# Weight buffers kept through the output projection, the first pair's weights loaded during it, and banks of their own for its first products

## The chip, the cores and the metric

The kernel runs on one core of a Trainium2 chip. The metric is the device time of one execution in microseconds (us); lower is better. The tensor engine is called PE, the vector engine DVE, the scalar engine ACT, GpSimd POOL, and SyncE, which here only issues transfers, SP.

## What is computed

One layer of a decoder step for 512 prompt rows and 8 x 4 sample rows, 544 columns in all, in 32-bit floats. The parts that matter here, cut from the reference:

```python
def mixer_block(h, pos, gla_s0, k_hist, v_hist, w_in, w_gate_up, b_gate, gla_norm, w_out):
    q_a, k_a, v_a, r_a, z_a, q_b, k_b, v_b = split_in_proj(h @ w_in)
    o_a, s_fin = gla_recurrence(...)
    gate = jax.nn.silu(r_a...)
    o_a = (rmsnorm(o_a, gla_norm) * gate)
    o_b = dilated_attention(...)
    y = jnp.concatenate([o_a, o_b], axis=-1) @ w_out

def conv_ffn(h, conv_hist, w_up, conv_w, conv_b, w_down):
    up = h @ w_up
    conv = conv_b + (causal convolution of width 3 over up)
    u, g = conv[..., :D_FF], conv[..., D_FF:]
    return (jax.nn.silu(g) * u) @ w_down

hp = hp + mixer(rmsnorm(hp, norm_mix));  hp = hp + conv_ffn(rmsnorm(hp, norm_ffn));  y = rmsnorm(hp, norm_final)
```

D_MODEL is 2048, D_FF 5504, w_in 2048 x 6160, w_out 2048 x 2048, w_up 2048 x 11008, w_down 5504 x 2048.

## The kernel before

Everything lies feature-major: a tile is 128 features by 544 columns, which `hv` shows as two halves of 272. A product is made of three matmuls of 128x272 per 128x128 block of weights: operands are split into a high part that the engine's fast 32-bit form keeps exactly and a low rest (`split`: ACT copies the high part, DVE subtracts), and high x high, high x low and low x high are added up (`gemm`, L225). Weights come in units of eight blocks: SP loads them into a `raw` buffer, ACT makes `whi` (L190), DVE `wlo` (L191).

The stages run one after the other:

- **Mixer.** Products with w_in, tile by tile, with the two attentions between them. Weight units lie in the pool `wts` (`raw`, `whi` and `wlo` with three buffers each; `wunit`). The last tiles are the gates of the heads (`in_tile(C_RA + ...)`, evaluated at L373 and in `silu_neg`); the last chunk of the gated attention (L762 to L769) ends at the same time, and L805 multiplies both.
- **Output projection.** `o` is split into `og` (L190, L191: `ah`, `al`), sixteen output tiles of two units each are multiplied, k in the order 10 to 15, 0 to 9, so that the heads finished last come last. Each tile is added to x (POOL loads x), written to `hscr` by POOL, squared for the norm's sum (L905, L906) and scaled (L908). Weight units lie in a second pool, `wu`, which is opened when `wts` is closed (L810, L811), with three `raw` and four `whi` and `wlo` buffers.
- **Factors and norm.** From two scaled tiles, `factors` builds the operands of a fast scheme for 2x2 blocks, which needs seven products where the plain one needs eight: `v` (L877) and `vh`, `vl` (L869, L870). The first four pairs of tiles are done as the projection goes, the last four after it (L914). `rms_stat` makes the norm's factor (L325 on PE, L167 to L171) in the banks of `pss`.
- **Up projection.** 43 pairs of tiles (`Pair`). For each, SP loads `ra` and `rs` into a pool `ra` with two buffers, POOL adds a second half of weights to them on the way in (L968), and further units go through `wraw`. `p1` is a product with plain 32-bit matmuls (L943), the other six are split ones (L938), into banks `b0` (two), `z` (two) and `y` (two) of the pool `psu`. That pool is opened when the norm's pool `pss` and the projection's `psg` are closed (L916, L920). The pools `ra` and `vb` take the place of `acts`, the split activations, and open when the projection is through (L911).
- **Down projection.** The last three finished pairs are kept on the chip and multiplied first, 18 matmuls for each of 16 output tiles, and ACT copies the result out (`h<-g`, L1129): the *kept phase*. The other 40 row tiles come back from memory in groups of 16, 16 and 8 (`fetch`, split by ACT and DVE as `dh`, `dl`). The last eight output tiles of the last group are done by halves, so that the final norm of one half can run beside the products of the other (`finish`, L1194; L1221 multiplies by the norm's factor). Its banks are new pools: three pairs `g`, two `v`.

Each engine runs its instructions in one fixed order. That order is made when the kernel is built, from priorities: code inside `high_priority` (`wpart`, `ahead`) is moved forward by up to a set distance. A buffer is given out again when all who used it have finished, and a pool that is opened in the place of another waits for the users of that other one.

Of the kernel before, what the change touches and what calls it, by code (L numbers as in the profile page):

```python
# [9 lines left out]
F32 = mybir.dt.float32  # L10
F32R = mybir.dt.float32r
U8 = mybir.dt.uint8
AF = mybir.ActivationFunctionType
OP = mybir.AluOpType
AX = mybir.AxisListType
PSUM = bass.MemoryType.PSUM

P = 128
D = 2048
KD = D // P  # L20
TP = 512
NB = 8
TS = 4
NS = NB * TS
NT = TP + NS
HT = NT // 2
NIN = 6160
C_QA, C_KA, C_VA, C_RA, C_Z, C_QB, C_KB, C_VB = 0, 640, 1280, 2560, 3840, 3856, 4624, 5392
RANK = 16
# [6 lines left out]
KF = FF // P  # L36
# [8 lines left out]
NKEPT = 3  # L45
NSLOT = 11
FW = 2 + TP + NB * (2 + TS)
# [62 lines left out]
NVEC = 54 + 258 + 86  # L110
# [13 lines left out]
def _build(tc, nc, es, xT, st_gla, ck, cv, conv_in, vecs, w_in, w_gu, w_out, w_up, w_dn,  # L124
           t_cs, t_bp, t_masks, t_scan, t_small,
           yT, gla_p, gla_s, kT_p, k_s, vT_p, v_s, conv_out):
    def opened(*args, **kw):
        p = tc.tile_pool(*args, **kw)
        return p, p.__enter__()

    def closed(*pools):
        for p in pools:
            p.__exit__(None, None, None)
# [25 lines left out]
    b_x = small[:NS, P + 25:P + 25 + TS * NB].rearrange("p (t b) -> p t b", t=TS)  # L159
    onesD = cons.tile([P, P], F32, name="onesD")  # L160
    eps = cons.tile([P, 1], F32, name="eps")
    zs = cons.tile([2 * RANK, NT], F32, name="zs")
    rstd = cons.tile([P, NT], F32, name="rstd")

    def rsqrt(dst, src, x, r):
# [71 lines left out]
    def ttile(name, dt=F32):  # L237
        return PA.tile([P, NT], dt, tag="T", name=name, bufs=5)

    phase = {"attention": True, "scores": False, "units": 0}  # L240
    nc.scalar.preload_act_table_set("natural_log_exp_and_others")
    xg = []
    acc = ttile("acc")
# [53 lines left out]
    def gps():  # L297
        return pg.tile([P, 2, 512], F32, tag="g", name="g")
# [4 lines left out]
    def vps():  # L303
        return pS.tile([P, 512], F32, tag="v", name="v", bufs=1)
# [502 lines left out]
    gl.__exit__(None, None, None)  # L807
    pe.__exit__(None, None, None)

    closed(wts_p)  # L810
    wu_p, wu = opened(name="wu", bufs=1, side="right")  # L811


    def wsplit(raw, n=8):

        hi = wu.tile([P, 8, P], F32R, tag="whi", name="whi", bufs=4)
        lo = wu.tile([P, 8, P], F32R, tag="wlo", name="wlo", bufs=4)
        split(hi[:, :n], lo[:, :n], raw[:, :n])
        return hi, lo

# [19 lines left out]
        return [(k, hi[:, i, :], lo[:, i, :]) for i, k in enumerate(ks)]  # L840

    def wraw():
        return wu.tile([P, 8, P], F32, tag="raw", name="raw", bufs=3)

    order = [10, 11, 12, 13, 14, 15, 0, 1, 2, 3, 4, 5, 6, 7, 8, 9]
    og = [None] * KD
# [3 lines left out]
    closed(rb2, rowsB_p, rowsA_p)  # L850

    va_p, VA = opened(name="va", bufs=1, side="right")
    hx_p, HX = opened(name="hx", bufs=1, side="right")
    hscr = [dram.tile([P, NT], F32, name=f"hscr{k}") for k in range(KD)]
    adr = [dram.tile([P, NT], F32, name=f"adr{k}") for k in range(KF)]
# [35 lines left out]
    for ot in range(KD):  # L891
# [17 lines left out]
        if j == 1 and i < AHEAD:  # L909
            factors([i], X, VA)  # L910
    closed(acts_p)  # L911
    ra_p, RA = opened(name="ra", bufs=2)
    vb_p, VB = opened(name="vb", bufs=1)
    factors(list(range(AHEAD, KD // 2)), X, VB)  # L914
    rms_stat(acc2, rstd, htmp)
    closed(hx_p, pss, psg)  # L916

    g0_p, G0 = opened(name="g0", bufs=NKEPT, side="right")
    fp_p, FP = opened(name="ffn", bufs=1, side="right")
    psu_p, pu = opened(name="psu", bufs=1, space=PSUM)  # L920
    rstdF = FP.tile([P, FW], F32, name="rstdF")
    nc.vector.memset(rstdF, 1.0)
    nc.scalar.activation(rstdF[:, 2:2 + TP], rstd[:, :TP], AF.Copy)
    nc.scalar.activation(rstdF[:, 2 + TP:].rearrange("p (b s) -> p b s", s=2 + TS)[:, :, 2:],
                         rstd[:, TP:].rearrange("p (b t) -> p b t", t=TS), AF.Copy)
    vcv = FP.tile([P, NVEC - V_CW], F32, name="vcv")
    nc.gpsimd.dma_start(vcv, vecs[:, V_CW:])
    wv = w_up.rearrange("(k t p) c -> t p k c", t=2, p=P)
    NP = TP - HT

# [12 lines left out]
            nc.tensor.matmul(b[:, :HT], a[:, i, :], v11[i], start=(i == 0), stop=(i == 7), skip_group_check=True)  # L943

    def tmp(name):
        return FP.tile([P, HT], F32, tag=name, name=name, bufs=1)

    def second(F, a, b):

        nc.vector.tensor_add(F[:, 2 + HT:2 + TP], a[:, :NP], b[:, :NP])  # L950
        nc.vector.tensor_add(F[:, 2 + TP:].rearrange("p (b s) -> p b s", s=2 + TS)[:, :, 2:],
                             a[:, NP:HT].rearrange("p (b t) -> p b t", t=TS), b[:, NP:HT].rearrange("p (b t) -> p b t", t=TS))

    class Pair:

# [3 lines left out]

        def load(self, *parts, tag=None):  # L960

            x = RA.tile([P, 8, P], F32, tag=tag, name=tag) if tag else wraw()
            for n, (side, t) in enumerate(parts):
                c0 = side * FF + self.f * P
                if n == 0:
                    nc.sync.dma_start(x, wv[t][:, :, c0:c0 + P])
                else:
                    nc.gpsimd.dma_start(x, wv[t][:, :, c0:c0 + P], accum_op=OP.add)  # L968
            return x
# [9 lines left out]
        def p5(self):  # L979
            with ahead():  # L980
                self.s = self.load((1, 0), (1, 1), tag="rs")
                A = wsplit(self.s)
            self.z = pu.tile([P, 512], F32, tag="z", name="z", bufs=2)
            product(self.z, A, T1)

        def p6(self):
# [7 lines left out]
        def p2(self):  # L994
            with ahead():
                self.a12 = self.load((0, 1))
                A = wsplit(self.a12)
                nc.vector.tensor_add(self.s, self.s, self.a12)
            y = pu.tile([P, 512], F32, tag="y", name="y", bufs=2)
            product(y, A, B21)  # L1000
            self.Fu, self.Fg = [FP.tile([P, FW], F32, tag="F", name="F", bufs=2) for _ in range(2)]
            for s, F in enumerate((self.Fu, self.Fg)):
                nc.gpsimd.memset(F[:, 0:2], 0.0)
                nc.scalar.activation(F[:, 2 + TP:].rearrange("p (b s) -> p b s", s=2 + TS)[:, :, 0:2],
                                     self.ci[:, s].rearrange("p (b r) -> p b r", r=2), AF.Copy, scale=(1.0, -1.0)[s])
            nc.vector.tensor_add(self.Fu[:, 2:2 + HT], y[:, :HT], self.V)
# [25 lines left out]
        def conv(self):  # L1032
# [12 lines left out]
                out.append(c)  # L1045
            return out

    ci_v = conv_in.rearrange("p (s f) r -> p s f r", s=2)
    co_v = conv_out.rearrange("p (s f) r -> p s f r", s=2)
    def sv(x):  # L1050
# [2 lines left out]
    KEPT = list(range(KF - 1 - NKEPT, KF - 1))  # L1053
    kept = {}
    ci = co = None
    pairs = [Pair(f) for f in range(KF)]
    for f, pr in enumerate(pairs):
        if f % 4 == 0:
            n = min(4, KF - f)
# [1 line left out]
            co = FP.tile([P, 2, 4, 2 + 2 * NB], F32, tag="co", name="co", bufs=2)  # L1061
            nc.gpsimd.dma_start(ci[:, :, :n, :], ci_v[:, :, f:f + n, :])
        pr.ci, pr.co = ci[:, :, f % 4, :], co[:, :, f % 4, :]
        if f == 0:
            pr.p1()
        pr.p5()
        pr.p6()
        pr.p2()
# [18 lines left out]
        if f % 4 == 3 or f == KF - 1:  # L1087
            f4 = f - f % 4
            nc.gpsimd.dma_start(co_v[:, :, f4:f + 1, :], co[:, :, :f + 1 - f4, :])
    closed(fp_p, vb_p, ra_p, psu_p)  # L1090


    rows_p, rows = opened(name="rows", bufs=KD)
    ds_p, DS = opened(name="ds", bufs=NSLOT)
    psd_p, pg = opened(name="psd", bufs=3, space=PSUM)
    psv_p, pS = opened(name="psv", bufs=2, space=PSUM)

    def vps():
        return pS.tile([P, 512], F32, tag="v", name="v")

    def gps():
        return pg.tile([P, 2, 512], F32, tag="g", name="g")

    taken = [0]

# [19 lines left out]
    for ot in range(KD):  # L1125
# [1 line left out]
        gemm(ps, [wpart(w_dn, KEPT, ot * P)], kept)  # L1127
        h[ot] = rows.tile([P, NT], F32, tag="R", name="h")
        nc.scalar.activation(hv(h[ot]), ps[:, :, :HT], AF.Copy)  # L1129
    closed(g0_p, va_p)  # L1130
    ds2_p, DS2 = opened(name="ds2", bufs=24 - NSLOT, side="right")
    w3_p, W3 = opened(name="w3", bufs=1, side="right")
    even = [0]
# [1 line left out]
    def wraw():  # L1135
        even[0] ^= 1
        if even[0]:
            return wu.tile([P, 8, P], F32, tag="raw", name="raw", bufs=3)
        return W3.tile([P, 8, P], F32, tag="raw3", name="raw3", bufs=2)

    def ctile(name):
# [71 lines left out]
    for s in range(2):  # L1213
# [5 lines left out]
        for ot in range(KD):  # L1219
            eng = nc.gpsimd if ot % 3 == 2 else nc.vector  # L1220
            eng.tensor_mul(h[ot][:, c], h[ot][:, c], rstd[:, c])  # L1221
            (nc.sync if ot % 2 else nc.scalar).dma_start(yT[ot * P:(ot + 1) * P, c], h[ot][:, c])
    closed(w3_p, ds2_p, ds_p, rows_p, wu_p, psv_p, psd_p)


# [64 lines left out]
```

## Time and profile before

| | |
|---|---|
| three runs | 2598.33, 2594.02, 2590.86 us; median 2594.02 |
| the profiled execution | 2600.62 us, of which its span is 2598.8 |
| PE busy | 2515.1 us, 97% of the span |
| DVE, ACT, POOL busy | 60%, 40%, 17% |
| mean granted clock of PE | 0.985 of 2.4 GHz |

An execution's time is its span and 1.8 us around it. The clock of PE has two levels, 2.4 and 1.2 GHz; the profile gives the granted one as a share of the higher. In a timeline row the bracket at the end tells how long the engine had been idle before the row and what released it; DMA-issuing rows of an engine's queue have a q behind its name.

### The profile page before, as it was taken

To read this page: it belongs to the slowest core of one execution; us is meant where nothing else is said; L and a number is where in the kernel's file an instruction comes from. 1 tells how busy PE (TensorE), PEld (TensorE's weight loads), DVE (VectorE), ACT (ScalarE), POOL (GpSimd) and SP (SyncE) were. 2 spreads that over 40 slices of the span, in tenths; PEclk is the share of its full clock that TensorE was granted. 3 is DMA by queue.
4 is the path that set the end of the run, shared out by engine and by line. 5 is a ranking of instruction groups with operands and counts; after the bars stand their busy time and mean duration, and the time that the engine had idled before them with its cause. 6 is when DMAs were issued, how large, how long until landed. Compare 5 with 4: busy or idle time off the path is not lost.

```text
span 2598.8 us, 46302 instructions
## 1 busy us (share of the span) xinstructions
PE 2515.1 (97%) x19135; PEld 2390.4 (92%) x19135; DVE 1570.1 (60%) x2381; ACT 1030.5 (40%) x1777; POOL 452.3 (17%) x592
## 2 busy tenths in 40 slices
PE   7999999999999699979999999999999999999997
PEld 7988877899998599979999999999999999999997
DVE  7877753267767644277777777777777653342244
ACT  5344454133334433244444444444444441131142
POOL 4433333300002300012122212121211000000001
PEclk9999999999999899989999999999999999999999
DMA  7777634622222253379999999999988384353332
GB/s 206 203 204 202 184 108 116 167 75 80 60 77 63 81 148 114 99 164 238 269 242 271 244 268 244 272 243 271 243 185 183 93 242 116 110 157 90 90 90 70
DMA packets 581588, 427.67 MB, mean 165 GB/s; under 512 B 18976, under 2 KB 553728, under 8 KB 580608
## 3 DMA queue, kind: packets, MB, share of 16 engines
q1 hardware_dynamic: 462144, 248.31, 34.7%
q0 software_dynamic: 115200, 171.02, 28.8%
q10 hardware_dynamic: 4032, 5.38, 0.6%
q8 instruction: 150, 2.46, 0.4%
q14 instruction: 62, 0.51, 0.1%
HBM read 397.40 MB, written 77.37 MB: 183 GB/s over the span
## 4 chain that ended last, share of the span: by engine, by line
PE 86%; DMA 6%; DVE 4%; issue 1%; ACT 1%; POOL 0%; SPq 0%; DVEq 0%; POOLq 0%; ACTq 0%
PE g L225 42%; PE b L938 15%; PE z L938 10%; PE b L943 6%; PE y L938 5%; DMA q<-qscr 4%; PE s L660 1%; PE v L507 1%; DMA ar<-adr 1%; PE s L555 1%; PE s L542 1%; DVE pr L411 1%; PE s L778 0%; PE s L781 0%; DMA rs<-in_w_up_dram 0%
## 5 line engine op out<-in xcount | busy, mean ns | idle before, releaser
L190 ACT ACTIVATE whi<-raw 128x1024 fp32r<-128x1024 f32 (+1 forms) x345 | 356.0, 1033 | 702.0 <-PE g L225 470.4
L191 DVE TENSOR_TENSOR wlo<-raw,whi 128x1024 fp32r<-128x1024 f32 (+1 forms) x341 | 408.2, 1198 | 216.7 <-ACT whi L190 208.4
L225 PE MATMUL g<-ah,whi 128*128 128x272 f32 x2048 | 442.4, 295 | 22.2 <-DMA raw<-in_w_out_dram 19.5
L225 PE MATMUL g<-ah,wlo 128*128 128x272 f32 x2048 | 442.9, 294 | 0.3 <-DVE wlo L191 0.3
L225 PE MATMUL g<-al,whi 128*128 128x272 f32 x2048 | 442.9, 295 | 0.0
L225 PEld LDWEIGHTS g<-ah,whi 128*128 128x128 f32 x2048 | 326.6, 190 | 36.9 <-ACT whi L190 22.0
L225 PEld LDWEIGHTS g<-ah,wlo 128*128 128x128 f32 x2048 | 328.1, 191 | 12.2 <-issue 10.1
L225 PEld LDWEIGHTS g<-al,whi 128*128 128x128 f32 x2048 | 327.8, 191 | 12.1 <-issue 10.4
L938 PE MATMUL b<-vh,whi 128*128 128x272 f32 x1032 | 306.3, 297 | 1.3 <-ACT V L1013 1.3
L938 PE MATMUL b<-vh,wlo 128*128 128x272 f32 x1032 | 296.9, 288 | 0.0
L938 PE MATMUL b<-vl,whi 128*128 128x272 f32 x1032 | 296.6, 287 | 0.0
L225 PE MATMUL g<-dh,whi 128*128 128x272 f32 x1248 | 258.5, 289 | 3.3 <-ACT whi L190 2.1
L225 PE MATMUL g<-dl,whi 128*128 128x272 f32 x1248 | 257.9, 288 | 0.0
L225 PE MATMUL g<-dh,wlo 128*128 128x272 f32 x1248 | 257.8, 288 | 0.0
L190 ACT ACTIVATE whi<-rs 128x1024 fp32r<-128x1024 f32 x129 | 135.9, 1054 | 193.8 <-PE b L938 123.6
L191 DVE TENSOR_TENSOR wlo<-rs,whi 128x1024 fp32r<-128x1024 f32 x129 | 157.7, 1222 | 84.5 <-ACT whi L190 84.5
L938 PE MATMUL z<-vh,whi 128*128 128x272 f32 x688 | 207.0, 301 | 0.0
L225 PEld LDWEIGHTS g<-dh,whi 128*128 128x128 f32 x1248 | 195.3, 188 | 4.2 <-ACT whi L190 2.5
L938 PE MATMUL z<-vh,wlo 128*128 128x272 f32 x688 | 198.5, 289 | 0.0
L938 PE MATMUL z<-vl,whi 128*128 128x272 f32 x688 | 198.1, 288 | 0.0
L938 PEld LDWEIGHTS b<-vh,whi 128*128 128x128 f32 x1032 | 194.9, 189 | 3.2 <-ACT V L1013 1.5
L938 PEld LDWEIGHTS b<-vl,whi 128*128 128x128 f32 x1032 | 194.4, 188 | 1.6
(347 smaller groups left out, 4699.0 us busy)
## 6 DMA issues: line engine op xcount, KB each, us to landing
raw<-in_w_up_dram SPq DMA_DIRECT2D x129, 512.0 KB, 5.4
raw<-in_w_in_dram SPq DMA_DIRECT2D x96, 512.0 KB, 4.3
raw<-in_w_dn_dram SPq DMA_DIRECT2D x64, 512.0 KB, 4.2
out_k_s_dram<-in_ck_dram POOLq DMA_DIRECT2D x8, 3060.0 KB, 17.0
out_v_s_dram<-in_cv_dram POOLq DMA_DIRECT2D x8, 3060.0 KB, 17.5
raw<-in_w_up_dram POOLq DMA_DIRECT2D x43, 512.0 KB, 7.7
ra<-in_w_up_dram SPq DMA_DIRECT2D x43, 512.0 KB, 7.6
rs<-in_w_up_dram SPq DMA_DIRECT2D x43, 512.0 KB, 6.4
```

The source lines that it names most:

```text
L190: nc.scalar.activation(hi, src, AF.Copy)
L191: eng.tensor_sub(lo, src, hi.bitcast(F32))
L225: nc.tensor.matmul(ps[:, s, :HT], a, b[:, s * HT:(s + 1) * HT], start=(i == 0 and n == 0), stop=(i == len(todo) - 1 and n == 2))
L411: nc.vector.tensor_mul(pr, kt[:, 4:5, :].broadcast_to([P, TS, QC]), q5[:, 1:5, :])
L507: nc.tensor.matmul(psv[32 * m:32 * m + 32, :QC], lhs, rhs, start=(kt == 0), stop=(kt == 5), tile_position=(0, 32 * m))
L542: nc.tensor.matmul(psc[:, :n], q[r, qi * P:(qi + 1) * P], k[r, :n], start=True, stop=True)
L555: nc.tensor.matmul(psc[r, :P], vt[:, j * P + 64 * e:j * P + 64 * e + 64], t[:, j * P:(j + 1) * P], start=(j == 0), stop=(j == qi))
L660: nc.tensor.matmul(ps[:, c * P:(c + 1) * P], KS[:, c * P:(c + 1) * P], Q[:, :, c * 64:(c + 1) * 64], start=True, stop=True)
L938: nc.tensor.matmul(b[:, :HT], a_[:, i, :], x_[i][:, v, :], start=(first and i == 0 and n == 0), stop=(i == 7 and n == 2), skip_group_check ...
L943: nc.tensor.matmul(b[:, :HT], a[:, i, :], v11[i], start=(i == 0), stop=(i == 7), skip_group_check=True)
```

## The change

It does six things, all in where buffers lie and in when code stands:

1. The pool `wts` isn't closed ahead of the output projection; `wraw` and `wsplit` take their buffers from it to the end of the kernel. `whi` and `wlo` then have three buffers where they had four. In the up projection every fourth unit's split goes to `xhi`, `xlo` in the pool `ra` instead, so that there are four in turn again.
2. The pool `pss` is closed before the output projection and `psu` opened there, with the banks `b0` (two) and one bank `v`, which the norm uses from then on, in the down projection too.
3. `psg`, the two bank pairs `g` of the mixer and the projection, stays to the end. `z` and `y` of a pair are the two halves of one such `g`; the down projection's tiles use `g` too, two pairs where they had three.
4. A pool `re` with one buffer for each of `ra` and `rs` is opened before the projection; even pairs use it, odd pairs the pool `ra`, which has one buffer now.
5. The first pair's `p1` (with its loads) stands ahead of the norm in the code; with `ahead` its loads and splits move into the projection.
6. `zs`, `V` and `U` lie in other pools.

```diff
@@ before the output projection @@
-    closed(wts_p)
     wu_p, wu = opened(name="wu", bufs=1, side="right")
     def wsplit(raw, n=8):
-        hi = wu.tile([P, 8, P], F32R, tag="whi", name="whi", bufs=4)
-        lo = wu.tile([P, 8, P], F32R, tag="wlo", name="wlo", bufs=4)
+        phase["units"] += 1
+        if phase["up"] and phase["units"] % 4 == 0:
+            hi = RA.tile([P, 8, P], F32R, name="xhi")
+            lo = RA.tile([P, 8, P], F32R, name="xlo")
+        else:
+            hi = wts.tile([P, 8, P], F32R, tag="whi", name="whi")
+            lo = wts.tile([P, 8, P], F32R, tag="wlo", name="wlo")
         split(hi[:, :n], lo[:, :n], raw[:, :n])
...
     def wraw():
-        return wu.tile([P, 8, P], F32, tag="raw", name="raw", bufs=3)
+        return wts.tile([P, 8, P], F32, tag="raw", name="raw", bufs=3)
+    closed(pss)
+    psu_p, pu = opened(name="psu", bufs=1, space=PSUM)
+    def vps():
+        return pu.tile([P, 512], F32, tag="v", name="v")
...
     va_p, VA = opened(name="va", bufs=1, side="right")
+    re_p, RE = opened(name="re", bufs=1, side="right")
     hx_p, HX = opened(name="hx", bufs=1, side="right")
@@ between output projection and up projection @@
     closed(acts_p)
-    ra_p, RA = opened(name="ra", bufs=2)
+    ra_p, RA = opened(name="ra", bufs=1)
     vb_p, VB = opened(name="vb", bufs=1)
     factors(list(range(AHEAD, KD // 2)), X, VB)
-    rms_stat(acc2, rstd, htmp)
-    closed(hx_p, pss, psg)
-    g0_p, G0 = opened(name="g0", bufs=NKEPT, side="right")
-    fp_p, FP = opened(name="ffn", bufs=1, side="right")
-    psu_p, pu = opened(name="psu", bufs=1, space=PSUM)
...
+    phase["up"], phase["units"] = True, 0
...
-            x = RA.tile([P, 8, P], F32, tag=tag, name=tag) if tag else wraw()
+            x = (RA if self.f % 2 else RE).tile([P, 8, P], F32, tag=tag, name=tag) if tag else wraw()
...
-            self.z = pu.tile([P, 512], F32, tag="z", name="z", bufs=2)
+            self.g = gps()
+            self.z = self.g[:, 0]
...
-            y = pu.tile([P, 512], F32, tag="y", name="y", bufs=2)
+            y = self.g[:, 1]
...
+    pairs = [Pair(f) for f in range(KF)]
+    pairs[0].p1()
+    rms_stat(acc2, rstd, htmp)
+    closed(hx_p)
+    g0_p, G0 = opened(name="g0", bufs=NKEPT, side="right")
+    fp_p, FP = opened(name="ffn", bufs=1, side="right")
...
-        if f == 0:
-            pr.p1()
@@ down projection @@
-    closed(fp_p, vb_p, ra_p, psu_p)
+    closed(fp_p, vb_p, ra_p)
+    phase["up"] = False
...
-    psd_p, pg = opened(name="psd", bufs=3, space=PSUM)
-    psv_p, pS = opened(name="psv", bufs=2, space=PSUM)
-    def vps():
-        return pS.tile([P, 512], F32, tag="v", name="v")
-    def gps():
-        return pg.tile([P, 2, 512], F32, tag="g", name="g")
```

What this does to the order of PE's rows at the two places. Between the last gate tile (`g<-ah_202`) and the output projection (`ah_9096`, its first operand, k = 10), before:

```order
L225 MATMUL g<-ah_202,wlo 128x272 x2
L764 MATMUL s<-sq,onesV 128x512
L778 MATMUL s<-ST,V 128x128 x2
L781 MATMUL s<-qe,S 128x128
L778 MATMUL s<-ST,V 128x128
L781 MATMUL s<-qe,S 128x128
L778 MATMUL s<-ST,V 128x128
L781 MATMUL s<-qe,S 128x128
L764 MATMUL s<-sq,onesV 128x512
L764 MATMUL s<-sq,onesV 128x64
L225 MATMUL g<-ah_9096,whi 128x272 x2
```

All of the attention's small matmuls stood ahead of the first product with w_out. PE at the same place in the changed kernel (`ah_9099` is k = 10 there, `ah_9111` k = 13):

```order
L225 MATMUL g<-ah_9111,whi 128x272 x2
L225 MATMUL g<-al_9112,whi 128x272 x2
L225 MATMUL g<-ah_9111,wlo 128x272
L764 MATMUL s<-sq,onesV 128x512
L778 MATMUL s<-ST,V 128x128 x2
L781 MATMUL s<-qe,S 128x128
L778 MATMUL s<-ST,V 128x128
L781 MATMUL s<-qe,S 128x128
L778 MATMUL s<-ST,V 128x128
L781 MATMUL s<-qe,S 128x128
L225 MATMUL g<-ah_9111,wlo 128x272
L225 MATMUL g<-ah_9115,whi 128x272 x2
```

The small matmuls now stand among the first tile's products, the first of them after four blocks of k; the two later L764 come after eight and thirteen blocks.

Between the output projection and the first pair, PE before (`v` is the norm's bank, `b_11281` the first pair's `b0`):

```order
L225 MATMUL g<-ah_9156,wlo 128x272 x2
L325 MATMUL v<-acc_9228,onesD 128x272 x2
L943 MATMUL b_11281<-v_9464,ra 128x272
L943 MATMUL b_11281<-v_9715,ra 128x272
L943 MATMUL b_11281<-v_9966,ra 128x272
```

The norm's two matmuls stood ahead of everything of the first pair. The same place of PE in the changed kernel (`b_11250` is the first pair's `b0`, `g` its `z`):

```order
L225 MATMUL g<-ah_9159,wlo 128x272 x2
L942 MATMUL b_11250<-v_9470,ra 128x272
L942 MATMUL b_11250<-v_9721,ra 128x272
L942 MATMUL b_11250<-v_9972,ra 128x272
L942 MATMUL b_11250<-v_10223,ra 128x272
L937 MATMUL g<-vh_9468,whi 128x272
L937 MATMUL g<-vl_9469,whi 128x272
```

The first pair's products come right behind the projection, with the operands of the first four pairs of tiles. The norm's matmuls stand 30 and 51 rows further on, the second pair's `p1` (`b_11432`) before them.

## Rows read from the trace of the kernel before

**Rows 1.** The page: busy time by engine, and one group of instructions.

```profile
PE 2515.1 (97%) x19135; PEld 2390.4 (92%) x19135; DVE 1570.1 (60%) x2381; ACT 1030.5 (40%) x1777; POOL 452.3 (17%) x592
...
L191 DVE TENSOR_TENSOR wlo<-raw,whi 128x1024 fp32r<-128x1024 f32 (+1 forms) x341 | 408.2, 1198 | 216.7 <-ACT whi L190 208.4
```

**Rows 2.** Stretches: from:to, length, busy time (count) by engine, clock, DMA.

```profile
880.00:906.00 26.00, 4.26 (x19) 2.48 (x17) 13.10 (x22) 9.08 (x18) 9.93 (x13) 0.66 0.51 162
906.00:1102.00 196.00, 195.98 (x1536) 195.45 (x1536) 74.44 (x93) 61.76 (x77) 13.12 (x22) 0.98 0.42 121
1102.00:1122.00 20.00, 2.88 (x6) 1.33 (x6) 15.56 (x30) 12.56 (x23) 3.72 (x3) 0.61 0.86 172
...
1141.00:2061.00 920.00, 918.39 (x6769) 891.72 (x6768) 656.23 (x934) 426.19 (x766) 178.58 (x239) 1.00 0.99 233
2061.00:2118.00 57.00, 54.18 (x413) 53.55 (x413) 27.08 (x41) 30.48 (x54) 1.32 (x2) 0.97 0.76 216
2118.00:2562.00 444.00, 443.81 (x3546) 443.73 (x3547) 159.37 (x187) 115.13 (x142) 0.00 (x0) 1.00 0.37 108
```

**Rows 3.** Timeline of PE, 880 to 910: start, duration, engine, line, operation.

```profile
886.16 0.41 PE L764 MATMUL s<-sq,onesV 128*128 128x64 f32 x2 [1.62 <-DVE oa L769]
906.02 0.82 PE L225 MATMUL g<-ah,whi 128*128 128x272 f32 x2 [19.45 <-DMA raw<-in_w_out_dram]
...
909.26 0.65 PE L225 MATMUL g<-ah,whi 128*128 128x272 f32 x2
909.71 0.66 PE L225 MATMUL g<-al,whi 128*128 128x272 f32 x2
```

**Rows 4.** Timeline of SP's queue and of DVE at 893.

```profile
893.00 22.38 SPq L830 DMA_DIRECT2D raw<-in_w_out_dram  x11
...
893.00 1.36 DVE L191 TENSOR_TENSOR al<-oa,ah 128x544 fp32r<-128x544 f32 x2
```

**Rows 5.** Chain of waits in 880 to 915 and in 1100 to 1145: start, duration, what.

```profile
897.98 8.05 DMA raw<-in_w_out_dram
...
1109.03 6.44 DMA rs<-in_w_up_dram
```

**Rows 6.** ACT's waits, 880 to 1102: total, times, longest.

```profile
ACT h L908 <- DMA hscr<-h: 41.3, 15, 9.7
```

**Rows 7.** Timeline of PE behind the output projection.

```profile
1109.02 1.28 PE L325 MATMUL v<-acc,onesD 128*128 128x272 f32 x2 [7.01 <-DVE acc L906]
...
1121.67 6.57 PE L943 MATMUL b<-v,ra 128*128 128x272 f32 x16 [7.68 <-DVE rs L169]
...
1141.94 1.99 PE L943 MATMUL b<-v,ra 128*128 128x272 f32 x8
```

**Rows 8.** Timeline of ACT and DVE behind the output projection.

```profile
1108.78 0.75 ACT L908 ACTIVATE h<-h,vec 128x544 f32<-128x544 f32 x1 [0.40 <-DMA hscr<-h]
...
1115.49 1.06 ACT L190 ACTIVATE whi<-rs 128x1024 fp32r<-128x1024 f32 x1 [3.89 <-DMA rs<-in_w_up_dram]
...
1128.12 0.72 DVE L870 TENSOR_TENSOR vl<-tu,vh 128x544 fp32r<-128x544 f32 x1
```

**Rows 9.** Timeline of DVE and PE in the up projection, at one pair.

```profile
1607.11 0.18 DVE L951 TENSOR_TENSOR F<-z,U 128x32 f32<-128x32 f32 x1
...
1621.71 0.49 PE L938 MATMUL z<-vh,whi 128*128 128x272 f32 x1
```

**Rows 10.** Timeline of PE and ACT in the kept phase.

```profile
2061.36 0.49 PE L225 MATMUL g<-dh,whi 128*128 128x272 f32 x2 [0.64 <-PE z L938]
...
2087.52 0.61 ACT L1129 ACTIVATE h<-g 128x544 f32<-128x544 f32 x1
```

**Rows 11.** Timeline of DVE at the last halves of output tiles.

```profile
2566.47 6.61 DVE L1221 TENSOR_TENSOR h<-h,rstd 128x272 f32<-128x272 f32 x11
...
2573.35 0.78 DVE L1194 TENSOR_TENSOR h<-h,g 128x272 f32<-128x272 f32 x2
2575.12 0.44 DVE L1194 TENSOR_TENSOR h<-h,g 128x272 f32<-128x272 f32 x1 [0.99 <-PE g L225]
```

## What the change is predicted to do

> **What bounds the kernel now.** I read the page first: PE is busy 97% of the span [rows 1], so time is won only where PE waits or runs slowly, and lost wherever PE is made to wait. The table by stretches then says where that is [rows 2]. In the up projection (1141 to 2061) PE works 918.4 of 920 us and in the down projection after 2118 443.8 of 444, at clock 1.00; the output projection (906 to 1102) has no gap. Two short stretches are nearly empty: 880 to 906, between the last gate product and the output projection (4.3 of 26 us busy, clock 0.66), and 1102 to 1122, between the output projection and the first pair of the up projection (2.9 of 20 us, clock 0.61). The change works on these two. The kept phase (2061 to 2118, 54.2 of 57 us) and the last tiles are where it takes something away.
>
> A matmul of 128x272 costs 443.81/3546 = 0.1252 us at the full clock [rows 2]; at the lower level two of them start 0.45 us apart, 0.226 each [rows 3].
>
> **First boundary: gates to output projection.** PE's idle 19.45 us before 906.02 ended with a load of w_out [rows 3]. The chain says why: the buffers of the mixer's weights are closed as a pool, so SP issues the first w_out load at 893.00, after the last split of the attention output (the DVE row of 893.00 is that work); the load that PE waited for was 8.05 us under way [rows 4, 5]. The change keeps the pool. The w_out loads then wait only for a raw buffer that w_in's last splits leave, and three of the first splits stand on ACT and DVE inside the gate tail. PE's rows, which are quoted with the change, go from the last gate product straight into k = 10 to 15, 0 to 7 of the first tile and 8 rows of k of the second, before they ask for og[8] and og[9], which the tail makes last. That is 22 steps of k, 6 matmuls each: 132 x 0.1252 = 16.5 us of work, with the 4.3 us of small matmuls among it, so PE is covered to about 20.8 us after the last gate product, which ends near 879.1 (the tail's small matmuls follow, to 886.57 [rows 3]): to 899.9. The tail ended at 893.00 + 1.36 = 894.4 [rows 4]. Added to it are splits, three on ACT and three on DVE, at 1.20 each by the slower of the two [rows 1]: 7.2 us if all six lie on the chain, 3.6 if every other one does: 898.0 to 901.6. I take 898.0, since ACT and DVE have gaps in the tail; then PE doesn't wait.
> What goes: 19.45 of idle, the wait of 1.62 inside the tail [rows 3], and the slow start: 1536 matmuls took 195.98 us in their stretch [rows 2] against 1536 x 0.1252 = 192.3, 3.7 us. Together 24.8. At the other end PE waits 1.7 us for og and pays part of a slow start once more, 2: 24.8 - 1.7 - 2 = 21. I take **-24.5**.
> Queues: SP's loads for pair 0 (ra, rs) now stand after seven w_out units and wait for the end of the attention's pools, about 898; units eight and later are needed 40 us after that, so nothing is late. POOL's accumulating half of rs stands behind ten loads of x rows and ahead of the writes of h; it waits for SP's half, and the first write follows at about 906, no earlier than its h. The projection splits its weights with 3 buffers in place of 4: the next split may start 12 us ahead of need, not 18. ACT's longest wait for something else there is 9.7 us [rows 6], and the two halves of a split take 2.4; 12.1 together, and the wait begins behind a split, so that nearly 18 are free. I cost it nothing; uncovered, it costs what lies above 12, here 0.1.
>
> **Second boundary: output projection to up projection.** Before, PE does the statistics at 1109.02, waits, and does pair 0's first products from 1121.67 on, 6.57 us for 16 records at the lower clock; the 8 records that end at 1143.93 take 1.99 [rows 7]. The chain runs through the two halves of rs, the second 6.44 us under way [rows 5], with ACT waiting 3.89 us for it and the factors queued behind [rows 8], and through the banks: the new pool opens when the statistics have been read. From 1102.0 to 1143.9, 41.9 us, PE did 4 x 1.99 = 8.0 us of first products, four products of 24 matmuls, 12.0, and 1.3 of statistics: 21.3. At most 20.6 can be won.
> Now ra and rs are there, their splits stand in the projection's last 12 us, and PE goes on with pair 0 in separate banks. What is late next is the factors of the last two output tiles: the scaled h comes at 1108.78, 6.8 us after the projection, and the last factor at 1128.12 + 0.72, 26.8 us after it [rows 8]. I followed ACT's and DVE's new rows with these durations, without the wait of 3.89, the 1.06 of its split, and the splits and additions of pair 0 on DVE: the last factor comes at 20.9. After it stand half a product's end, y and one more product, 6.5 us: 27.4, against 41.9, a gain of 14.5. With factors as late as now it is 33.3, a gain of 8.6. PE works in pieces until then and may well restart at the lower clock: two products at 0.226 cost 4.9 more, half of it 2.5. Pair 1's ra is loaded only after the projection; PE stands before it, but the factors are later. I take **-12**, between 4 (factors late and slow clock) and 14.5.
>
> **Up projection.** The rows of all engines are in the same order here; three weight buffers plus one in a freed place are again four in turn, RE and RA are again two. z and y share a tile: z of the next pair but one starts 14.4 us after the last read of z (1607.29 to 1621.71 [rows 9]). **0**.
>
> **Down projection.** Two bank pairs in place of three. A kept tile is 18 matmuls, 2.25 us, and tile n + 2 may start only when tile n has been copied out by ACT, which stands among the splits of reloaded rows. The tenth tile ends about 2061.4 + 22.6 = 2083.9 (the first starts at 2061.36); its copy ran 2087.52 to 2088.13 [rows 10], and the twelfth started at 2086.2: 1.9 us late with two. The others come out within 0.3. **+2**, between 0 (PE is idle 2.8 us in this phase already [rows 2], mostly for weights that then come while it waits) and 5 (the clock falls for a few us).
> Tiles of the later groups take 6 us and more and their copies come at once; nothing. At the end the tiles are halves of 24 matmuls, 3.0 us. DVE does eleven multiplications in a row from 2566.47 and only then, at 2573.35, copies out the two halves that wait [rows 11]; the half that ends at 2575.1 started at 2572.1. With two pairs it needs the first copy, done at 2573.7. **+1.7**, on the path to the end; 3.3 if the clock falls.
>
> Sum: -24.5 - 12 + 2 + 1.7 = **-32.8**. The profiled execution took 2600.6, 6.6 more than the median of 2594.0: 2567.8 for it, 2561 for the median.
>
> A row and a rule on the bank pairs: the projection ran 196 us with two pairs and no gap, at clock 0.98 [rows 2], with tiles of 12 us. The Trainium skill ("TensorE: Matmul & The Clock Gate", section "A second HAM failure mode: psum-queue depth-cycling") tells of a kernel in which cycling through the banks made PE idle briefly between groups, so that its clock kept falling and rising. Here that speaks against two pairs for 2.25 us tiles; the present kept phase, with three, shows no such fall (clock 0.97).
>
> **Rivals.**
> (a) The second boundary stays bound by the late factors and the clock: -4 in place of -12, 2569. For it: 19 us from the scaled h to the last factor now. Against: ACT stood idle 3.89 of them.
> (b) The first weights still come late, because the raw buffers are released by the last splits of w_in or the tail is lengthened beyond the cover: the first boundary gives 10, 2575. Against: w_in's own loads keep PE fed by the same buffers until the last gate product.
> (c) PE waits a little at each kept tile and its clock falls for the phase: 288 matmuls x (0.226 - 0.125) = 29 us in place of 2, 2588. Against: most copies come in time. This is the mechanism of the rule above.
> (d) Slower: the shared tile of z and y holds back each pair. It decides once the last read comes over 14.4 us later than now [rows 9], and each us beyond costs 41 pairs x 1 us; at 1.0 beyond, 2561 + 41 = 2602. Against: the order is the same, and PE is idle 1.6 us in the whole stretch [rows 2].
> (e) The pools still wait as before, by another buffer in the same place, and nothing comes of it: 2594.
>
> **How the numbers follow.** About 0.3% (7.8 us) is what a measurement can tell from no change. Forecast 2561: 0.73; (a) 0.12; (b) 0.05; (c) 0.05; (d) 0.03; (e) 0.02. Faster: 0.73 + 0.12 + 0.05 = 0.90; same: (c) and (e), 0.07; slower: (d), 0.03. The range: the bounds of the terms give -25 - 14.5 + 0 + 1.7 = -38, 2556, and -21 - 4 + 5 + 3.3 = -17, 2577; with the spread of the runs, 2590.9 to 2598.3, on the lower side: 2551 to 2578, which holds the forecast and (a), and (b).
>
> **What would show it.** First boundary: no PE wait above 2 us between the last gate product and the second output tile, and 192 to 194 us of products at clock 1.00. Second: first products of pair 0 right behind the projection, the last factor about 21 us later, steady pairs from 27 to 30 us. Kept phase: one or two PE waits on ACT's copy of L1135 near the tenth to twelfth tile. End: a PE wait of 1.7 us on DVE's L1200. The period of a pair stays 21.7. The prediction is wrong if PE waits for og or w_out, if the period changes, or if the clock of the kept phase falls.

## The result

| | before | changed |
|---|---|---|
| median | 2595.4 us (4 runs, 2590.9 to 2598.3) | 2560.1 us (4 runs, 2558.6 to 2564.1) |
| the profiled execution | 2600.6, span 2598.8 | 2560.6, span 2558.8 |
| PE busy | 2515.1 us, 97% | 2510.5 us, 98% |

The ratio is 0.9868, with a 95% interval of 0.9849 to 0.9887: faster by 35 us, 29 to 39. The forecast was 2561, its range 2551 to 2578. Two later sets, each beside fresh runs of the kernel before, gave 0.9864 (0.9841 to 0.9887) and 0.9871 (0.9853 to 0.9889). One execution of a kernel below (the rest without the kept weights) took 3497.9 us at a granted clock of 0.65 and is left out of that kernel's figures.

The table by stretches of the changed kernel (from:to, length, busy time and count of PE, PEld, DVE, ACT and POOL, clock, DMA share, GB/s) answers to [rows 2]:

```profile
880.00:906.00 26.00, 26.00 (x195) 24.65 (x194) 15.84 (x24) 10.94 (x18) 11.80 (x15) 1.00 0.52 162
906.00:1074.00 168.00, 168.00 (x1340) 168.00 (x1339) 70.43 (x90) 56.71 (x74) 13.47 (x23) 1.00 0.49 135
1074.00:1094.00 20.00, 17.13 (x90) 14.57 (x89) 18.74 (x36) 15.34 (x27) 4.73 (x5) 0.90 0.93 198
...
1101.00:2021.00 920.00, 920.00 (x6789) 893.93 (x6789) 658.49 (x938) 428.68 (x771) 181.18 (x241) 1.00 0.98 232
2021.00:2078.00 57.00, 52.56 (x407) 51.12 (x406) 26.82 (x39) 29.50 (x50) 0.60 (x1) 1.00 0.74 216
2078.00:2521.00 443.00, 443.00 (x3538) 442.84 (x3537) 158.90 (x188) 115.82 (x144) 0.00 (x0) 1.00 0.38 109
2521.00:2558.80 37.80, 22.44 (x160) 21.36 (x158) 21.21 (x41) 7.40 (x17) 9.15 (x10) 0.81 0.34 119
```

880 to 906, where PE had 4.26 us of work at clock 0.66, is full at 1.00. The 20 us behind the output projection held 2.88 us of work and hold 17.13. The up projection is as it was.

**First boundary.** What SP's queue waited for in the kernel before (860 to 912: total, times, longest), and its timeline in the changed kernel:

```profile
SPq L830 <- DVE oa L805: 59.1, 1, 59.1
...
833.98 55.28 SPq L834 DMA_DIRECT2D raw<-in_w_out_dram  x11
896.00 0.37 SPq L967 DMA_DIRECT2D ra<-in_w_up_dram  x1
```

Before, SP stood 59.1 us behind the multiplication of L805 with the first w_out load. Now that load is issued at 833.98, 59 us ahead of [rows 4] and some 43 us before the gates' products end. L805 reads no weights: it reads `oa` and a gate `r`, which lies in the mixer's pool `pe`, closed at the same place in the code. So the load seems to have waited for the users of all that the new pool may cover, `pe` as well as `wts`. Whether a new pool that fits into the place of `wts` alone would have waited less no run shows. PE's rows there in the changed kernel:

```profile
879.16 0.29 PE L225 MATMUL g<-ah,wlo 128*128 128x272 f32 x1
879.29 1.02 PE L764 MATMUL s<-sq,onesV 128*128 128x512 f32 x2
...
886.64 1.02 PE L764 MATMUL s<-sq,onesV 128*128 128x512 f32 x2
...
890.89 0.33 PE L764 MATMUL s<-sq,onesV 128*128 128x64 f32 x2
```

Not one row carries a bracket. The waits of 1.62 and 19.45 in [rows 3] are gone, and the tail's small matmuls run between products of the projection. The tail ends soon enough; ACT's row for the last two high parts of `og`:

```profile
893.82 1.30 ACT L190 ACTIVATE ah<-oa 128x544 fp32r<-128x544 f32 x2 [1.96 <-DVE oa L805]
```

**Second boundary.** PE's rows where [rows 7] had its two waits of 7 us:

```profile
1073.66 0.41 PE L225 MATMUL g<-ah,wlo 128*128 128x272 f32 x2
1073.91 2.00 PE L942 MATMUL b<-v,ra 128*128 128x272 f32 x8
...
1077.25 5.21 PE L942 MATMUL b<-v,ra 128*128 128x272 f32 x22
...
1083.25 0.62 PE L325 MATMUL v<-acc,onesD 128*128 128x272 f32 x2
...
1090.82 0.59 PE L937 MATMUL g<-vh,whi 128*128 128x272 f32 x1 [1.95 <-ACT vh L880]
...
1097.69 0.29 PE L937 MATMUL b<-vh,xhi 128*128 128x272 f32 x1
```

The first pair's product starts where the projection ends, the second pair's stands 3.3 us behind it, the norm's matmuls fit in between, and the longest wait left is 1.95 us for a late factor.

### The profile page after: what moved, and what is told of

Read it like the earlier page. It is cut to its first block, busy times and chain, and to the rows that moved or that the text cites. A ratio compares the mean times of both kernels' runs of the same rounds, so it can differ in the third digit from the quotient of the medians.

```text
span 2558.8 us, 46323 instructions
## 1 busy us (share of the span) xinstructions
PE 2510.5 (98%) x19135; PEld 2387.8 (93%) x19135; DVE 1569.8 (61%) x2381; ACT 1031.4 (40%) x1777; POOL 455.2 (18%) x592
## 4 chain that ended last, share of the span: by engine, by line
PE 86%; DMA 5%; DVE 4%; issue 1%; ACT 1%; POOL 0%; SPq 0%; DVEq 0%; POOLq 0%; ACTq 0%
PE g L225 42%; PE g L937 15%; PE b L937 15%; PE b L942 6%; DMA q<-qscr 4%; DMA ar<-adr 1%; PE s L660 1%; PE v L507 1%; PE s L555 1%; PE s L542 1%; DVE pr L411 1%; PE s L778 1%; PE s L781 0%; DVE h L1227 0%; PE s L552 0%
## 5 line engine op out<-in xcount | busy, mean ns | idle before, releaser
L191 DVE TENSOR_TENSOR wlo<-raw,whi 128x1024 fp32r<-128x1024 f32 (+1 forms) x298 | 356.0, 1196 | 207.5 <-ACT whi L190 200.2
L937 PE MATMUL g<-vh,whi 128*128 128x272 f32 x1032 | 307.5, 298 | 2.2 <-ACT vh L880 2.2
L937 PE MATMUL g<-vl,whi 128*128 128x272 f32 x1032 | 298.9, 290 | 0.7 <-DVE vl L881 0.7
L937 PE MATMUL g<-vh,wlo 128*128 128x272 f32 x1032 | 298.2, 289 | 0.0
L937 PEld LDWEIGHTS g<-vh,whi 128*128 128x128 f32 x1032 | 195.4, 189 | 4.5 <-ACT vh L880 2.8
L937 PEld LDWEIGHTS g<-vl,whi 128*128 128x128 f32 x1032 | 195.3, 189 | 2.9 <-DVE vl L881 1.2
L225 PEld LDWEIGHTS g<-dh,wlo 128*128 128x128 f32 x1248 | 195.3, 188 | 0.2 <-DVE wlo L191 0.2
L937 PEld LDWEIGHTS g<-vh,wlo 128*128 128x128 f32 x1032 | 195.1, 189 | 0.0
L225 PEld LDWEIGHTS g<-dl,whi 128*128 128x128 f32 x1248 | 195.1, 188 | 0.0
L942 PE MATMUL b<-v,ra 128*128 128x272 f32 x688 | 171.4, 392 | 0.0
```

Source lines behind the costliest of these rows:

```text
L191: eng.tensor_sub(lo, src, hi.bitcast(F32))
L225: nc.tensor.matmul(ps[:, s, :HT], a, b[:, s * HT:(s + 1) * HT], start=(i == 0 and n == 0), stop=(i == len(todo) - 1 and n == 2))
L937: nc.tensor.matmul(b[:, :HT], a_[:, i, :], x_[i][:, v, :], start=(first and i == 0 and n == 0), stop=(i == 7 and n == 2), skip_group_check ...
```

## Experiments

Ratios are to the kernel before, which ran in the same set each time (medians 2593.0, 2593.4 and 2595.1). "Later" and "above" the changed kernel go by its profile above and by this second median of it, which comes from the first of these sets. The runs on the banks, the loads and the cover are of the second set, in which the changed kernel did not run:

> The changed kernel as it is, beside the others on the same chip: 34 to 36 us less than before, about 2560.

Measured: 2560.4 us (2555.3 to 2561.7).

**One part alone: the weight buffers kept.** The kernel before, with `wts` left open; with it, as in the change, goes that `whi` and `wlo` have three buffers and that every fourth unit of the up projection is split into `xhi`, `xlo`.

```diff
-    closed(wts_p)
-    wu_p, wu = opened(name="wu", bufs=1, side="right")
+    phase["up"], phase["n"] = False, 0
 ...
-        hi = wu.tile([P, 8, P], F32R, tag="whi", name="whi", bufs=4)
+            hi = wts.tile([P, 8, P], F32R, tag="whi", name="whi")
```

> The kernel before with one part of the change: the mixers' weight buffers are kept to the end (three whi and wlo, every fourth unit of the up projection in xhi, xlo); the first pair and all banks are as before. Theory (the two boundaries add up, and the first is worth the idle of 19.45, the wait of 1.62 and the slow start of 3.7): 25 us less than before, about 2570, no PE wait above 2 us between the last gate product and the second output tile, and the waits of 7.0, 2.4 and 7.7 us behind the output projection as they were. Rival (the attention's tail binds PE, not the loads): PE still waits over 5 us for og, and the gain is 10 to 18 us.

Measured: 2572.4 us (2568.8 to 2577.6), ratio 0.9909 (0.9882 to 0.9936). The table by stretches of this kernel, over the first boundary:

```profile
878.00:906.00 28.00, 28.00 (x206) 26.20 (x207) 19.29 (x29) 13.93 (x22) 11.72 (x15) 1.00 0.41 117
```

and its PE rows behind the projection:

```profile
1076.00 0.41 PE L225 MATMUL g<-ah,wlo 128*128 128x272 f32 x2
1084.42 1.25 PE L325 MATMUL v<-acc,onesD 128*128 128x272 f32 x2 [8.01 <-issue]
1087.69 1.27 PE L325 MATMUL v<-acc,onesD 128*128 128x272 f32 x2 [2.02 <-DVE rs L169]
1096.86 6.53 PE L947 MATMUL b<-v,ra 128*128 128x272 f32 x16 [7.89 <-issue]
```

The first boundary is full by this part alone, and the second stands nearly as in [rows 7], with waits of 8.0, 2.0 and 7.9 where there were 7.0, 2.4 and 7.7. So the kept pool brings the whole gain of the first: 20.6 us by the medians (17 to 31 by the interval), 25.6 by the ends of the projection in the two traces (1102.0 and 1076.4), which had reached the evaluation of the last gate within 0.3 us of each other (L373 at 879.38 and 879.61).

**The rest without it.** The changed kernel, with `wts` closed again and a new pool of three buffers each.

```diff
-    wu_p, wu = opened(name="wu", bufs=1, side="right")
+    closed(wts_p)
+    wu_p, wu = opened(name="wu", bufs=3, side="right")
 ...
-            hi = wts.tile([P, 8, P], F32R, tag="whi", name="whi")
+            hi = wu.tile([P, 8, P], F32R, tag="whi", name="whi")
```

> The changed kernel without that part: the mixers' weight pool is closed ahead of the output projection again, with a second pool of three buffers in its place; the first pair's early loads, its banks, and two bank pairs in the down projection are as in the changed kernel. Theory: the first boundary's idle of 19 to 20 us is back, the second gains 15 us (from the end of the projection to the end of the first six products 27 us in place of 42), and the kept phase and the end lose 2 and 3.6: 2595 - 15 + 3 to 6, about 2584 to 2587. Rival (the two parts depend on one another, the early loads of pair 0 stand in SP's queue in the way of w_out): the first boundary's idle grows by 3 us or more, and the time is 2588 or above.

Measured: 2583.4 us (2577.0 to 2586.9), ratio 0.9956 (0.9939 to 0.9973). With the 0.9909 of the run above this makes 0.91% and 0.44%, and the whole change took 1.36% in the same set: the two parts add up. PE's rows at both boundaries:

```profile
901.59 0.82 PE L225 MATMUL g<-ah,whi 128*128 128x272 f32 x2 [15.14 <-ACT whi L190]
...
1097.66 2.00 PE L943 MATMUL b<-v,ra 128*128 128x272 f32 x8
...
1120.71 0.29 PE L938 MATMUL b<-vh,xhi 128*128 128x272 f32 x1
```

The idle time at the first boundary is back, 15.1 in place of 19.45; the second boundary is as in the changed kernel: the `xhi` product starts 23.1 us after the projection's end, there 23.8. From the end of the idle time to the end of the projection it is 196.2 us, in before 196.0: pair 0's loads, which stand in SP's queue among those of w_out, cost the projection next to nothing (0.2 us). That rival falls.

**The banks back behind the norm.** The changed kernel with `psu` opened, and `pairs[0].p1()` called, after `rms_stat`.

```diff
-    closed(pss)
-    psu_p, pu = opened(name="psu", bufs=1, space=PSUM)
 ...
-    pairs[0].p1()
     rms_stat(acc2, rstd, htmp)
+    closed(pss)
+    psu_p, pu = opened(name="psu", bufs=1, space=PSUM)
+    pairs[0].p1()
```

> The changed kernel with the banks b0 opened only when the norm has been read, as before, and the first pair's code behind the norm; its weights still come during the projection, and z has its bank. Theory (the banks are worth about as much as the early loads): the first products start at the norm's second L169, some 15 us after the projection, and 8 us of first products with 3 of another product follow, partly at the lower clock; the sixth product ends 7 to 10 us later than in the changed kernel: about 2568. Rival 1 (the early loads do it all): within 2 us of the changed kernel. Rival 2 (the banks do it all): 15 us later, 2575.

Measured: 2566.7 us (2561.7 to 2568.2), ratio 0.9887 (0.9869 to 0.9906). Its PE rows behind the projection, which ends at 1072.24:

```profile
1076.08 0.39 PE L931 MATMUL g<-vh,whi 128*128 128x272 f32 x1 [2.18 <-ACT vh L874]
...
1080.99 0.60 PE L931 MATMUL g<-vh,whi 128*128 128x272 f32 x1 [3.63 <-ACT vh L874]
...
1087.77 7.04 PE L936 MATMUL b<-v,ra 128*128 128x272 f32 x22 [0.52 <-DVE rs L169]
...
1103.14 0.49 PE L931 MATMUL b<-vh,xhi 128*128 128x272 f32 x1
```

The products that filled the time up to the factors now come behind them. The `xhi` product starts 30.9 us after the projection, 7.1 later than in the changed kernel.

**The loads back behind the projection.** The changed kernel with the pool `re` opened where `ra` is.

```diff
-    re_p, RE = opened(name="re", bufs=1, side="right")
 ...
     closed(acts_p)
+    re_p, RE = opened(name="re", bufs=1)
     ra_p, RA = opened(name="ra", bufs=1)
```

> The changed kernel with the first pair's ra and rs in a pool that opens only behind the projection, as before; banks and code as in the changed kernel. Theory: ra lands about 6 us and the second half of rs 13 us after the projection, ACT waits for it with the factors queued behind; the sixth product ends 4 to 8 us later than in the changed kernel: about 2566. Rival 1 (the banks do it all): within 2 us. Rival 2 (the loads do it all): 15 us later, 2575.

Measured: 2562.8 us (2560.9 to 2570.1), ratio 0.9873 (0.9853 to 0.9893): above the changed kernel by 2.4, which the spread of the runs covers. The trace is clearer; PE behind the projection, which ends at 1078.5:

```profile
1082.94 9.26 PE L942 MATMUL b<-v,ra 128*128 128x272 f32 x32 [4.29 <-DMA ra<-in_w_up_dram]
...
1093.39 0.39 PE L937 MATMUL g<-vh,whi 128*128 128x272 f32 x1 [0.72 <-ACT whi L190]
...
1106.09 0.29 PE L937 MATMUL b<-vh,xhi 128*128 128x272 f32 x1
```

PE waits 4.29 us for `ra`, but then has 32 matmuls in a row, the `p1` of two pairs, while rs is loaded and split. The `xhi` product starts 27.6 us after the projection, 3.8 later than in the changed kernel. I expected more here. The two parts don't add up to the second boundary's gain (7.1 and 3.8 of 15): each alone still fills part of the time up to the factors.

**The cover taken away.** The changed kernel, whose output projection begins with the two k that the gate tail makes last.

```diff
-    order = [10, 11, 12, 13, 14, 15, 0, 1, 2, 3, 4, 5, 6, 7, 8, 9]
+    order = [8, 9, 10, 11, 12, 13, 14, 15, 0, 1, 2, 3, 4, 5, 6, 7]
```

> The changed kernel with the k order of the output projection begun with 8 and 9, the two heads that the attention's tail finishes last, in place of ended with them. Theory (early weights are worth 25 us only because PE has 22 steps of k to do while the tail runs): PE asks for og[8] 8 us after the last gate product and gets it 13 to 15 us after it; 5 to 7 us of idle, 2 us of waits of the small matmuls that stand in a row again, and a slow start of 3 to 4: 10 to 13 us more than the changed kernel, about 2572. Rival (the loads alone were what PE waited for): within 3 us of the changed kernel.

Measured: 2573.9 us (2571.1 to 2575.1), ratio 0.9917 (0.99 to 0.9934), 13.5 us above the changed kernel. PE's rows:

```profile
883.24 1.76 PE L764 MATMUL s<-sq,onesV 128*128 128x512 f32 x2 [0.88 <-DVE sq L169]
885.99 0.66 PE L764 MATMUL s<-sq,onesV 128*128 128x64 f32 x2 [0.99 <-ACT sq L762]
893.11 1.27 PE L225 MATMUL g<-ah,whi 128*128 128x272 f32 x4 [6.46 <-ACT ah L190]
```

The loads are as early as in the changed kernel; what is missing is work for PE while the tail runs, and PE then works at the lower clock until 897. So the first boundary's gain needs both: weights that are there, and fourteen k that don't depend on the tail.

**A third bank pair in the down projection.** The changed kernel, with `psu` closed behind the up projection and a pool opened there that has one more `g`.

```diff
-    closed(fp_p, vb_p, ra_p)
+    closed(fp_p, vb_p, ra_p, psu_p)
     phase["up"] = False
+    psd_p, pd = opened(name="psd", bufs=1, space=PSUM)
+    def gps():
+        phase["g"] += 1
+        return (pg if phase["g"] % 3 else pd).tile([P, 2, 512], F32, tag="g", name="g")
```

> The changed kernel with a third bank pair in the down projection, in the banks that the up projection's b0 leaves. Theory (two pairs cost PE the wait of 1.75 us at the last halves and the lower clock behind it, 3.6 us in all, and 2 us of waits in the kept phase): 3 to 5 us less than the changed kernel, about 2556, no PE wait on L1200, none on L1135. Rival (DVE's eleven multiplications hold up the end anyway, so that what PE waits for is no loss): the same time as the changed kernel within 1 us.

Measured: 2555.3 us (2548.7 to 2559.2), ratio 0.9848 (0.9826 to 0.9871). Its runs overlap with those of the changed kernel, so both were run once more, side by side.

> The changed kernel again, beside the one with a third bank pair, to see whether the two differ by more than the spread of their runs. 2560, as in the two earlier sets.

> The changed kernel with a third bank pair in the down projection, again. If the two bank pairs cost what the two traces show, 2.1 us of PE waits in the kept phase and 3.6 at the end, this one is 5 us below the changed kernel, 2555. If the difference of the first set was spread of the runs, the two come within 2 us of each other.

Measured: 2559.7 (2556.3 to 2563.1) for the changed kernel, 2554.6 (2551.4 to 2555.9) with three pairs, ratios 0.9871 (0.9853 to 0.9889) and 0.9847 (0.9832 to 0.9862). The ranges no longer meet: three pairs are 5.1 us faster, and this is the fastest kernel of the study. DVE's rows at the last halves, of the changed kernel first:

```profile
2522.46 0.44 DVE L1200 TENSOR_TENSOR h<-h,g 128x272 f32<-128x272 f32 x1 [0.17 <-PE g L225]
2522.81 6.61 DVE L1227 TENSOR_TENSOR h<-h,rstd 128x272 f32<-128x272 f32 x11
...
2529.70 0.77 DVE L1200 TENSOR_TENSOR h<-h,g 128x272 f32<-128x272 f32 x2
2535.03 0.44 DVE L1200 TENSOR_TENSOR h<-h,g 128x272 f32<-128x272 f32 x1 [4.56 <-PE g L225]
```

and with three pairs:

```profile
2523.48 0.44 DVE L1209 TENSOR_TENSOR h<-h,g 128x272 f32<-128x272 f32 x1 [0.17 <-PE g L225]
2523.84 6.61 DVE L1236 TENSOR_TENSOR h<-h,rstd 128x272 f32<-128x272 f32 x11
...
2530.73 0.77 DVE L1209 TENSOR_TENSOR h<-h,g 128x272 f32<-128x272 f32 x2
2532.49 0.44 DVE L1209 TENSOR_TENSOR h<-h,g 128x272 f32<-128x272 f32 x1 [0.99 <-PE g L225]
```

From the copy ahead of the eleven multiplications to the third half behind them it is 12.57 us with two pairs and 9.01 with three, which is also the time in before (2566.11 to the 2575.12 of [rows 11]). From that first copy to the end of the span, the three traces of the changed kernel have 36.3, 36.5 and 36.4, the two with three pairs 33.2 and 33.1, before 32.7.

## Why the prediction was right

The two profiled spans differ by 40.0 us, and the places where the same work stands in both say where it went.

| stretch | predicted | from the traces |
|---|---|---|
| ahead of the change (784 to 806) | 0 | -3.0 |
| first boundary | -24.5 | -24.9 |
| second boundary | -12 | -15.1 |
| up projection and kept phase, to the first half of the end | +2 | -0.6 |
| end | +1.7 | +3.6 |
| sum | -32.8 | -40.0 |

**The 3.0 ahead of the change** is no gain. The code there is the same; the profiled execution of before ran a piece of it at the lower clock (last section). Without it the sum of the traces is -37.0, and the medians differ by 35.3, 32.6 and 35.4 in the three sets. It also says why the second line of my sum, from the profiled 2600.6 down to the median, was needed.

**First boundary: right.** The end of the projection moved from 1102.0 to 1074.1, 27.9 us, of which 3.0 are the piece above. Cover and tail came out as worked. The gates' products end at 876.6 here, and the high parts of the last `og` are ready at 895.1, its low parts at 895.9: 18.6 and 19.3 us behind them, where I took 18.9 (898.0 less 879.1). So the cover of 20.8 us had 1.5 to spare, PE didn't wait, and rival (b) fell. The run without cover shows that this term rested on the order of k, as the prediction had it.

Two readings in it were off, without harm to the sum. SP's first load of w_out waited for L805, not for the last split, which only starts at the same time. And PE's wait in before ended with ACT's split of the first unit, not with the load of 8.05 us; ACT's row:

```profile
904.91 2.00 ACT L190 ACTIVATE whi<-raw 128x1024 fp32r<-128x1024 f32 x2 [11.30 <-DMA raw<-in_w_out_dram]
```

**Second boundary: right mechanism, mis-sized term.** The end of the `xhi` product (1100.85), which answers to 1143.93 in [rows 7], is 43.08 us earlier; less the 27.93 of the projection's end, 15.15 are won, above my upper end of 14.5. The failing step was the one that I followed by hand: the last factor's row

```profile
1091.69 0.72 DVE L881 TENSOR_TENSOR vl<-tu,vh 128x544 fp32r<-128x544 f32 x1
```

ends 18.3 us after the projection, not 20.9, since the norm's and the factors' rows on DVE pack more closely than I had them: from 1077.73 up to this one they follow one another without an idle time. The rest, 0.6, is the lower clock, for which I took half of 4.9: once the last factor is there, PE's rows run at half pace from 1092.9 to 1096.9 only, some 18 matmuls at 0.227 in place of 0.125, 1.8 us. Rival (a), factors as late as before, fell with it. The split by experiments (banks 7, loads 4) wasn't in the prediction, which took them together.

**Up projection: right.** 920.00 busy of 920.00, the period of a pair is 21.73 us in both kernels, and rival (d), the shared tile of z and y, shows in no row. The output projection, with three weight buffers in place of four, is full too (168.00 of 168.00).

**Kept phase: the sum of the waits as forecast, their places in part.** PE's rows in the changed kernel:

```profile
2035.24 0.52 PE L225 MATMUL g<-dh,whi 128*128 128x272 f32 x2 [0.71 <-ACT h L1135]
...
2043.44 0.52 PE L225 MATMUL g<-dh,whi 128*128 128x272 f32 x2 [1.14 <-ACT h L1135]
...
2053.19 0.52 PE L225 MATMUL g<-dh,whi 128*128 128x272 f32 x2 [0.21 <-ACT h L1135]
```

They stand ahead of the ninth, twelfth and sixteenth tile and are 2.06 together, the +2 of the sum, and in two other traces of the same kernel 2.9 and 1.1; with three pairs there are none. I had worked out the twelfth alone, at 1.9, and none above 0.3 elsewhere; that 1.14, 0.71 and 0.21 make the same sum is luck. From the `xhi` product to the first half of the end the traces take 1424.8, 1427.0 and 1424.8 with two pairs, 1423.3 and 1424.0 with three: 1.9 apart in the mean. The line of the table shows -0.6, for the greater part since the one trace of before ran its kept phase at 0.97 [rows 2], this one at 1.00. Rival (c) fell: over this phase the three traces with two pairs show 1.00, 0.97 and 0.97, no less than before with three. A 0.97 is here one piece of 3.4 us at the lower level, and it doesn't stand behind these waits but, with two pairs and with three, behind PE's wait for weights at the phase's end (1.91 us in before, at 2105.77). The rule behind rival (c) (the Trainium skill, "TensorE: Matmul & The Clock Gate", section "A second HAM failure mode: psum-queue depth-cycling") tells of a clock that falls and rises again and again over frequent short idle times. The traces show none of that: the waits come ahead of one to three of the sixteen tiles, and behind the longest, 1.55 in the second trace, the matmuls go on at 0.125 us each.

**End: right wait, too small a price.** PE's rows in the changed kernel:

```profile
2528.14 0.29 PE L225 MATMUL g<-dh,dl 128*128 128x272 f32 x1
2530.18 0.39 PE L225 MATMUL g<-dh 128*128 128x272 f32 x1 [1.75 <-DVE h L1200]
...
2533.51 0.43 PE L225 MATMUL g<-dh 128*128 128x272 f32 x1
2533.73 0.37 PE L225 MATMUL g<-dl,dh 128*128 128x272 f32 x1
2533.94 0.29 PE L225 MATMUL g<-dh,dl 128*128 128x272 f32 x1
```

The wait is 1.75, for the copy that I named. But behind it the matmuls start 0.227 us apart up to 2533.9, the lower level, which costs another 1.8. The prediction had that as its other end, 3.3, and took the lower one. Here a single wait was followed by what those ahead of the kept tiles were not. The wait for weights at the end of the kept phase was followed by it in before (1.91 us) and in the other two traces of the changed kernel (2.39 and 2.47), and not in this one (2.12); what decides it no run shows.

The errors of the two mis-sized terms, -3.1 and +1.9, and that of the kept phase in this trace partly cancelled. The median came out at 2560 for a forecast of 2561, nearer than the terms were: that closeness is luck.

## What to carry to other kernels

Where a long idle stretch of the bottleneck ends with a load, look at when the load was issued and which buffer's place it waited for: a pool that is closed and replaced at the border of two stages can hold back the next stage's first loads until the last reader of something in that place is done, here one that reads no weights, and keeping the old pool was worth 25 us. Early weights only pay if there is work that doesn't depend on the tail; the order of k was worth half of it. Banks taken from one stage to feed another have a price where they are missed: give them back as soon as the stage is over, which was worth 5 us more.

## What the runs showed of the hardware beyond that

PE's clock falls for some us in the middle of stretches in which PE is never idle, in some executions and not in others. The table by stretches of before:

```profile
790.00:795.00 5.00, 5.00 (x22) 4.57 (x21) 0.00 (x0) 1.24 (x2) 4.45 (x4) 0.50 0.35 105
```

and of the changed kernel, same code and same place:

```profile
790.00:795.00 5.00, 5.00 (x35) 4.28 (x34) 0.00 (x0) 1.64 (x3) 4.42 (x5) 1.00 0.36 108
```

PE is busy 5.00 of 5.00 in both; one has the clock at 0.50 and does 22 matmuls, the other 35 at 1.00. Ahead of it stand the small matmuls of the gated attention, and the piece cost 3.0 us. The first profile with three pairs has another such piece: the clock is 0.83 in 560 to 580 with PE busy all 20 us, where the second profile of the changed kernel has 1.00. What sets it off stays open: no run here was made to tell. How many of these pieces an execution has may account for a good part of the 5 to 14 us by which the runs of one kernel differ: of fourteen runs of before in one set, the five shortest (2587.5 to 2591.1) have a mean granted clock of 0.988 or 0.989, the four longest (2598.7 to 2601.2) one of 0.985. This is why places in the trace had to be compared beside the medians.

With the new pool in place of the kept one, PE's first product with w_out came 4.4 us earlier than in before, at 901.59, although the loads were issued at the same time, 892.87 and 893.00. In both, SP issued five of them up to 898 and POOL eight loads of x rows beside them. ACT's first split, which PE waited for, began 11.9 us after the first issue in before (904.91) and 7.6 us after it with the new pool (900.48). Why is open; no run was made to tell.
